# Weights loaded in half-chunks, and experts' outputs scattered as rounded float32r with their remainders

## The chip, the cores and the metric

The kernel runs on one core of one Trainium2 chip. The metric is the device time of one execution in microseconds (us). The engines are named as in the profile: PE (TensorE matmul), PEld (its weight loads), DVE (VectorE), ACT (ScalarE), POOL (GpSimd), SP (SyncE, which issues the DMAs).

## The reference

Two transformer blocks on 256 tokens of width 2048, all float32: a convolution block with a dense FFN, and a gated block that ends in a mixture of experts. The change touches the mixture (and the way that all weights are loaded). What it computes, cut to what matters:

```python
# 16 experts in 4 groups; each token goes to the 2 best experts of its best group
hid = silu(einsum('td,edf->tef', t, w_gate)) * einsum('td,edf->tef', t, w_up)     # f = 512
y = einsum('tef,efd->td', hid * gate[:, :, None], w_down)                         # d = 2048
h = h + y
return rms_norm(h, norm_final_g)
```

## The kernel before

**Streams.** All weights come from HBM once, in one fixed order, as 1 MB chunks of 128 partitions x 2048 float32 (`Stream`, lines 50 to 104). `load` issues a chunk on SP's queue into one of 4 `raw` buffers. A chunk is used as two halves of 1024 columns. Each half is split in two float32r parts: `hi`, a rounded copy on ACT (L74), and `lo`, the difference on DVE (L83; on POOL for a few early chunks). A product with a float32 weight is then two or three float32r products. When the `lo` of a chunk's second half is issued, the buffer is given back and the next chunk is loaded into it. In the mixture, `take` keeps ACT 4 halves and DVE 3 halves ahead of PE (`MOE_HI, MOE_LO`), with 5 `hi` and 4 `lo` buffers.

**The mixture** (`experts`, L1079). Each expert has 64 slots. Its stage *in e* (`into`, L1212) takes 16 halves, each with four products of 512 columns, and gathers tokens four experts at a time: while *in 3*, *in 7* and *in 11* run, PE and ACT also gather the tokens of the next four. Its stage *down e* (`down`, L1190) takes 8 halves, again with four products each; after two halves a bank of 512 columns is complete and ACT copies it to `Yt` (L1203). The order of stages is in 0, in 1, down 0, in 2, down 1, in 3, down 2, ..., in 14, down 13, down 14, in 15, down 15. Between *in e* and *down e* lie seven small jobs (`between`, L1159: gate and up out of their banks `gu` on ACT, folded by PE, silu, product, split into `hd`), done one per half in the stage that follows *in e*.

**The scatter.** `scatter(k, es)` (L1141) adds the outputs of a pair of experts (e-1, e), e even, to the tokens for one block k of 128 features: for each expert one float32 product of 256 columns, with `Yt` as weights and `sc` (slots x tokens, carrying the gate and the norm) as the moving side, then one DVE addition into `h` (L1148). Experts 0 and 15 are scattered alone. The 16 scatters of a pair wait in `todo`; `fill` puts them on PE after the products of a half, so far as a credit of 0.5 us per half goes (`FILL_GU`, `FILL_DOWN`). `sc` is made per expert in `spread` (L1126) by two DVE instructions.

**Order.** Every engine executes its own instructions in the order in which the code emits them. `beat` (L1091) emits for each half: ACT's `hi` and DVE's `lo` that run ahead, then all that was posted before (reads of banks), then one job of `between`; then come PE's products of the half. So an ACT copy out of a bank stands in ACT's queue behind `hi` casts of later halves, which wait for their DMAs.

Of the kernel before, what the change touches and what calls it, by code (L numbers as in the profile page):

```python
# [7 lines left out]
F32 = mybir.dt.float32  # L8
F32R = mybir.dt.float32r
# [6 lines left out]
P = 128  # L16
# [24 lines left out]
RAW_BUFS, HI_BUFS, LO_BUFS = 4, 5, 4  # L41
# [7 lines left out]
class Stream:  # L49
# [9 lines left out]
    def load(self, upto):  # L59
        while self.loaded < min(upto, len(self.order)):  # L60
            t = self.raw.tile([P, 2048], F32, tag="raw", name=f"raw{self.loaded}")
            self.nc.sync.dma_start(out=t, in_=self.order[self.loaded][0])
            self.raws[self.loaded] = t
            self.loaded += 1

    def source(self, half):
        i, s = divmod(half, 2)
        self.load(i + 1)
        return self.raws[i][:, s * 1024 : (s + 1) * 1024]
# [8 lines left out]
    def low_to(self, halves):  # L78
        while self.n_low < halves:
            i, s = divmod(self.n_low, 2)  # L80
            eng = self.nc.gpsimd if self.order[i][1] else self.nc.vector
# [50 lines left out]
def network(ctx, tc, a, out):  # L132
# [62 lines left out]
    y = const.tile([P, KB, T], F32, name="y")  # L195
# [754 lines left out]
    lt = wE.tile([20, T], F32, name="lt")  # L950
# [125 lines left out]
    yx = wE.tile([P, 8, T], F32, name="yx")  # L1076
    Yt = [t.rearrange("p a t -> p (a t)") for t in (y[:, :8, :], y[:, 8:, :], yx)]

    def experts(hot, stream, extra):  # L1079
        scat, rsl, hids, left = {}, {}, {}, [0] * NE  # L1080
# [45 lines left out]
        def spread(e):  # L1126
# [4 lines left out]
            sc = wF.tile([P, T], F32, tag="sc", bufs=5, name=f"sc{e}_{turn_of[0]}")  # L1131
            rs = wF.tile([P, 1], F32, tag="rs", name=f"rs{e}_{turn_of[0]}")
# [6 lines left out]
            scat[e], rsl[e] = sc, rs  # L1139
# [198 lines left out]
```

## Time and profile before

| | us |
|---|---|
| median of 3 runs (2280.13 to 2283.72) | 2283.22 |
| the profiled execution | 2283.07 |
| its span | 2281.3 |

| engine, whole span | busy us | share |
|---|---|---|
| PE | 2219.8 | 97% |
| DVE | 1596.8 | 70% |
| ACT | 1255.5 | 55% |
| POOL | 214.6 | 9% |

Up to about 1680 us the kernel is dense (convolution, FFN, projections); the mixture with its 192 chunks takes from 1680 to 2260, the final norm and output the rest. The busy time of an engine is the union of its instructions; a wait is put down to the instruction that ended it. PE's matmuls are pipelined, so the cost of one is read from the distance between starts, not from its duration.

### The profile page before, as it was taken

How to read it: one execution, taken by the hardware profiler on the slowest of the kernel's cores; microseconds unless marked ns; L12 is line 12 of the kernel's file. 1: busy time of each engine (PE TensorE's matmuls, PEld its weight loads, DVE VectorE, ACT ScalarE, POOL GpSimd, SP SyncE). 2: the span in 40 equal slices, each digit the busy share in tenths (PEclk: the TensorE clock that was granted, in tenths of full speed). 3: DMA queues.
4: the chain of work that ended last, by engine and by line, in shares of the span. 5: the costliest groups of instructions: out<-in, count | busy, mean ns of one | idle time of the engine just before them, and what ended most of it. 6: DMA issues, size and time to landing. Idle time of an engine off the chain costs nothing. (4 is left out here: it accounts for less than half of the span.)

```text
span 2281.3 us, 40365 instructions
## 1 busy us (share of the span) xinstructions
PE 2219.8 (97%) x16539; PEld 2079.1 (91%) x16539; DVE 1596.8 (70%) x2259; ACT 1255.5 (55%) x1638; POOL 214.6 (9%) x162
## 2 busy tenths in 40 slices
PE   6999999999999999999999999999999999999996
PEld 6999899999999999999899999999976878778785
DVE  7999767655544455555875664566579899888996
ACT  4445555544434444444553444444577878778774
POOL 5798100000000000001100000000000000000001
PEclk8999999999999999999999999999999999999998
DMA  5444354555555555555655555555559999999993
GB/s 212 167 166 161 101 202 167 187 200 188 200 188 200 189 198 191 191 198 188 222 185 196 193 185 188 198 190 201 169 205 367 355 351 355 331 348 344 354 357 135
DMA packets 71410, 508.79 MB, mean 223 GB/s; under 512 B 7936, under 2 KB 7952, under 8 KB 10288
## 3 DMA queue, kind: packets, MB, share of 16 engines
q1 hardware_dynamic: 70560, 503.85, 62.3%
q8 instruction: 131, 2.15, 0.4%
q0 software_dynamic: 656, 2.27, 0.3%
q14 instruction: 63, 0.52, 0.1%
HBM read 503.99 MB, written 2.10 MB: 222 GB/s over the span
## 5 line engine op out<-in xcount | busy, mean ns | idle before, releaser
L83 DVE TENSOR_TENSOR lo<-raw,hi 128x1024 fp32r<-128x1024 f32 x884 | 1064.1, 1222 | 534.4 <-PE bank L165 471.9
L74 ACT CAST hi<-raw 128x1024 fp32r<-128x1024 f32 x952 | 986.4, 1054 | 770.5 <-PE bank L165 674.6
L165 PE MATMUL bank<-aH,hi 128*128 128x256 f32 (+1 forms) x3456 | 965.4, 280 | 7.1 <-ACT aH L244 5.3
L165 PE MATMUL bank<-aL,hi 128*128 128x256 f32 (+1 forms) x3456 | 960.0, 279 | 8.0 <-DVE aL L246 8.0
L165 PE MATMUL bank<-aH,lo 128*128 128x256 f32 (+1 forms) x3456 | 962.6, 279 | 0.4 <-DVE lo L83 0.4
L165 PEld LDWEIGHTS bank<-aH,hi 128*128 128x128 f32 x3456 | 652.7, 189 | 10.1 <-ACT aH L244 5.7
L165 PEld LDWEIGHTS bank<-aL,hi 128*128 128x128 f32 x3456 | 649.8, 189 | 9.5 <-DVE aL L246 9.3
L165 PEld LDWEIGHTS bank<-aH,lo 128*128 128x128 f32 x3456 | 652.4, 189 | 0.6 <-DVE lo L83 0.6
L536 POOL TENSOR_TENSOR acc<-acc,sq 128x256 f32<-128x256 f32 x23 | 17.7, 768 | 1925.3 <-ACT sq L677 722.9
L165 PE MATMUL bank<-hidH,lo 128*128 128x256 f32 x704 | 194.3, 276 | 0.0
L165 PE MATMUL bank<-hidH,hi 128*128 128x256 f32 x704 | 194.3, 276 | 0.0
L165 PE MATMUL bank<-hidL,hi 128*128 128x256 f32 x704 | 194.3, 276 | 0.0
L83 POOL TENSOR_TENSOR lo<-raw,hi 128x1024 fp32r<-128x1024 f32 x68 | 163.4, 2415 | 52.8 <-ACT hi L74 33.1
L285 DVE SCALAR_TENSOR_TENSOR bank<-glu,vec,bank 128x256 f32<-128x256 f32 x387 | 160.6, 483 | 1.9
L165 PEld LDWEIGHTS bank<-hidH,hi 128*128 128x128 f32 x704 | 132.2, 188 | 0.0
L165 PEld LDWEIGHTS bank<-hidL,hi 128*128 128x128 f32 x704 | 132.2, 188 | 0.0
L165 PEld LDWEIGHTS bank<-hidH,lo 128*128 128x128 f32 x704 | 132.2, 188 | 0.0
L165 PE MATMUL bank<-hi,aH 128*128 128x512 f32 x320 | 128.8, 419 | 1.1 <-ACT hi L74 0.8
L165 PE MATMUL bank<-hi,aL 128*128 128x512 f32 x320 | 126.2, 411 | 0.0
L165 PE MATMUL bank<-lo,aH 128*128 128x512 f32 x320 | 123.3, 401 | 2.0 <-DVE lo L83 2.0
L165 PE MATMUL bank<-hi,hd_first 128*128 128x512 f32 x256 | 112.3, 439 | 0.1
L165 PE MATMUL bank<-lo,aL 128*128 128x512 f32 x256 | 103.3, 404 | 1.7 <-DVE lo L83 1.4
(284 smaller groups left out, 2181.9 us busy)
## 6 DMA issues: line engine op xcount, KB each, us to landing
raw<-egu SPq DMA_DIRECT2D x128, 1024.0 KB, 5.2
raw<-gu SPq DMA_DIRECT2D x88, 1024.0 KB, 4.8
raw<-w SPq DMA_DIRECT2D x72, 1024.0 KB, 4.8
raw<-edn SPq DMA_DIRECT2D x64, 1024.0 KB, 5.8
raw<-dn SPq DMA_DIRECT2D x44, 1024.0 KB, 4.8
raw<-cw_in SPq DMA_DIRECT2D x32, 1024.0 KB, 4.8
raw<-cw_out SPq DMA_DIRECT2D x16, 1024.0 KB, 4.8
raw<-wup SPq DMA_DIRECT2D x16, 1024.0 KB, 4.8
```

The costliest lines, as they stand in the source:

```text
L74: self.nc.scalar.copy(hi, self.source(self.n_high))
L83: eng.tensor_tensor(lo, self.source(self.n_low), self.highs[self.n_low].bitcast(F32), OP.subtract)
L165: nc.tensor.matmul(o, l, r, start=start, stop=stop, skip_group_check=True)
L285: nc.vector.scalar_tensor_tensor(dw[:, j, :] if t == end - 1 else ta, gl, V("w_dw", j * TAPS + t), early[j % 2] if t == 1 else ta, OP.mult ...
L536: (nc.gpsimd if n or gpsimd else nc.vector).tensor_tensor(acc[:, n, :], acc[:, n, :], sq, OP.add)
```

## The change

It has three parts.

1. `Stream` loads halves (512 KB, 128 x 1024, rows of 4 KB out of rows of 8 KB) into 8 `raw` buffers instead of chunks into 4; a buffer is given back after the `lo` of its own half.
2. An expert's output is rounded to float32r when ACT copies it out of its bank to `Yt`. Half a step later PE adds, by a product with minus the identity, minus the rounded value to the bank, so that the bank keeps the remainder, and ACT copies the 64 rows that matter to `yl` (a pair shares it: one expert in rows 0 to 63, the other in 64 to 127; `hd` is laid out accordingly). A scatter does two feature blocks in one bank, all float32r: per block one product for each expert and one for both remainders, then one DVE addition of 512 columns.
3. `sc` becomes a matrix of 0 and 1; the gate goes into ACT's copy of `gu` instead. `spread` makes three DVE instructions of its two, and ACT copies half of `sc` to `both`, the moving side of the remainders. `Yt` has two buffers in the place of three, in the room of `y`; `FILL` credits are charged 0.72 for two blocks of a pair, where one block was charged 0.86.

```diff
-RAW_BUFS, HI_BUFS, LO_BUFS = 4, 5, 4
+RAW_BUFS, HI_BUFS, LO_BUFS = 8, 5, 4
...
+            t = self.raw.tile([P, 1024], F32, tag="raw", name=f"raw{self.loaded}")
+            self.nc.sync.dma_start(out=t, in_=self.order[i][0][:, s * 1024 : (s + 1) * 1024])
...
+            del self.raws[self.n_low]
             self.n_low += 1
-            if s == 1:
-                del self.raws[i]
-                self.load(i + 1 + RAW_BUFS)
+            self.load(self.n_low + RAW_BUFS)
...
             def scale():
-                nc.vector.scalar_tensor_tensor(sc, o[:, :T], slot_col, rb, OP.is_equal, OP.mult, accum_out=rs)
-                nc.vector.tensor_tensor(sc, o[:, T:], sc, OP.mult)
+                nc.vector.scalar_tensor_tensor(scaled, o[:, :T], slot_col, rb, OP.is_equal, OP.mult, accum_out=rs)
+                nc.vector.scalar_tensor_tensor(scaled, scaled, 1.0, o[:, T:], OP.mult, OP.mult, accum_out=gs)
+                nc.vector.tensor_scalar(sc, o[:, :T], slot_col, None, OP.is_equal)
+                nc.scalar.copy(pairs[e][high_rows(e), :], sc[high_rows(e), :].bitcast(F32))
...
         def scatter(k, es):
             b, o = spare()
-            for n, e in enumerate(es):
-                mm(o[:, :T], Yt[e % 3][:, k * P : (k + 1) * P], scat[e], n == 0, n == len(es) - 1)
-                left[e] -= 1
+            rows = slice(0, P) if len(es) == 2 else high_rows(es[0])
+            for kk in (k, k + 1):
+                sl, to = slice(kk * P, (kk + 1) * P), o[:, kk % 2 * T : (kk % 2 + 1) * T]
+                for n, e in enumerate(es):
+                    mm(to, Yt[e % 2][:, sl], scat[e], kk == k and n == 0, False)
+                mm(to, yl[rows, sl], pairs[es[0]][rows, :], False, True)
...
             def add():
-                nc.vector.tensor_tensor(h[:, k, :], h[:, k, :], o[:, :T], OP.add)
+                two = h[:, k : k + 2, :]
+                nc.vector.tensor_tensor(two, two, o.rearrange("p (a t) -> p a t", a=2), OP.add)
...
-                nc.scalar.copy(gu[:, 1, :], bank[1])
+                nc.scalar.activation(gu[:, 1, :], bank[1], ACT.Copy, scale=gsl[e])
...
-                        def out_of_bank(c=c, o=o):
-                            nc.scalar.copy(Yt[e % 3][:, c * 512 : (c + 1) * 512], o)
+                        def out_of_bank(c=c, o=o, sl=sl):
+                            nc.scalar.copy(Yt[e % 2][:, sl], o)
+                            post(lambda: lost(c, o, sl))
+                        def lost(c, o, sl):
+                            mm(o, minus, Yt[e % 2][:, sl], False, True)
+                            nc.scalar.copy(yl[rows, sl], o[rows])
                             es = (e,) if e in (0, NE - 1) else (e - 1, e)
                             if e == NE - 1 or e % 2 == 0:
-                                for k in range(4 * c, 4 * c + 4):
-                                    todo.append((0.43 * len(es), lambda k=k: scatter(k, es)))
+                                for k in (4 * c, 4 * c + 2):
+                                    todo.append((0.24 * (len(es) + 1), lambda k=k: scatter(k, es)))
```

**Where the instructions stand.** On PE in *down 6*, a stage whose pair begins to be scattered, before: `bank_62` and `bank_63` take the expert's output, `bank_66` and `bank_67` the scatters. Here the third and fourth halves:

```order
L165 MATMUL bank_63<-hi_20836,hd_first 128x512
L165 MATMUL bank_63<-lo_20856,hd_first 128x512
L165 MATMUL bank_66<-sc_first,yx 128x256
L165 MATMUL bank_66<-sc_first,y 128x256
L165 MATMUL bank_67<-sc_first,yx 128x256
L165 MATMUL bank_67<-sc_first,y 128x256
L165 MATMUL bank_63<-hi_20854,hd_first 128x512
```

The same place after:

```order
L164 MATMUL bank_63<-lo_21730,hd_first 128x512
L164 MATMUL bank_62<-Yt_first,minus 128x512
L164 MATMUL bank_63<-hi_21728,hd_first 128x512
L164 MATMUL bank_63<-lo_21743,hd_first 128x512
L164 MATMUL bank_63<-hi_21728,hd_first 128x512
L164 MATMUL bank_63<-lo_21743,hd_first 128x512
L164 MATMUL bank_66<-sc_first,Yt_first 128x256 x2
L164 MATMUL bank_66<-both_first,yl 128x256
L164 MATMUL bank_66<-sc_first,Yt_first 128x256 x2
L164 MATMUL bank_66<-both_first,yl 128x256
```

A product with `minus` now stands between two halves, and the scatters begin one half later, two blocks to a bank. Counted over the program, a *down* of an even expert (2 to 12) holds 5 blocks of a pair before and 10 after, the next *in* 9 and 6, the *down* of the odd expert behind it 2 and none; three `minus` products stand in each *down* and the fourth in the *in* that follows.

On ACT in the same stage, before, from the copies of `gu` on:

```order
L1164 COPY gu_first<-bank_61 128x512
L74 CAST hi_20865<-raw_20778 128x1024
L74 CAST hi_20879<-raw_20778 128x1024
L1203 COPY y<-bank_62 128x512
L74 CAST hi_20896<-raw_20806 128x1024
L1177 ACTIVATE sg_first<-bank_64 128x256
L74 CAST hi_20909<-raw_20806 128x1024
```

After:

```order
L1185 ACTIVATE gu_first<-bank_61,gs_first 128x512
L75 CAST hi_21741<-raw_21628 128x1024
L75 CAST hi_21755<-raw_21643 128x1024
L1228 CAST Yt_first<-bank_62 128x512
L75 CAST hi_21770<-raw_21658 128x1024
L1234 CAST yl<-bank_62 64x512
L1198 ACTIVATE sg_first<-bank_64 128x256
L75 CAST hi_21795<-raw_21673 128x1024
```

Behind each copy of an output, one `hi` cast later, a second read of the same bank (L1234) has come in.

## Rows read from the trace of the kernel before

**Rows 1.** Busy time by stage, eight windows in a row less the last: us, then engines
```profile
1841.64:1861.68 20.04, 19.00 (x69) 11.59 (x68) 18.59 (x17) 16.01 (x17) 0.00 (x0) 1.00 0.99 408
1861.68:1877.44 15.76, 13.74 (x70) 11.28 (x68) 14.04 (x20) 13.29 (x18) 0.00 (x0) 1.00 0.90 334
1877.44:1901.14 23.70, 23.70 (x106) 19.41 (x105) 22.89 (x29) 16.75 (x19) 0.00 (x0) 1.00 0.97 360
1901.14:1912.31 11.17, 11.17 (x58) 9.49 (x57) 9.09 (x13) 8.77 (x14) 0.00 (x0) 1.00 0.86 293
1912.31:1936.75 24.44, 23.96 (x134) 20.11 (x132) 22.55 (x24) 24.29 (x34) 0.00 (x0) 1.00 0.98 380
1936.75:1950.81 14.06, 13.65 (x70) 11.34 (x69) 11.09 (x15) 12.15 (x18) 0.00 (x0) 1.00 0.84 297
1950.81:1974.66 23.85, 23.85 (x107) 19.46 (x105) 22.91 (x29) 16.86 (x19) 0.00 (x0) 1.00 0.96 356
```

**Rows 2.** Timeline, PE: one block of a pair's scatter between plain products
```profile
1948.34 0.60 PE L165 MATMUL bank<-sc_first,yx 128*128 128x256 f32 x2
1948.78 0.59 PE L165 MATMUL bank<-sc_first,y 128*128 128x256 f32 x2
1949.02 0.58 PE L165 MATMUL bank<-hi,hd_first 128*128 128x512 f32 x1
1949.44 0.39 PE L165 MATMUL bank<-lo,hd_first 128*128 128x512 f32 x1
```

**Rows 3.** Timeline, PE: float32r products of 512 and of 256 columns
```profile
1688.72 0.39 PE L165 MATMUL bank<-lo,aH 128*128 128x512 f32 x1
1688.95 0.40 PE L165 MATMUL bank<-hot_first,tH 128*128 128x256 f32 x2
1689.19 0.40 PE L165 MATMUL bank<-hot_first,tL 128*128 128x256 f32 x2
```

**Rows 4.** Groups of instructions by line and shape: busy us, mean ns | idle before
```profile
L1148 DVE TENSOR_TENSOR x<-x,bank 128x256 f32<-128x256 f32 x144 | 59.7, 419 | 32.6 <-PE bank L165 31.4
L847 DVE TENSOR_TENSOR vm<-bank,bsb 128x512 f32<-128x512 f32 x4 | 2.8, 689 | 2.8 <-PE bank L165 2.7
L1203 ACT COPY y<-bank 128x512 f32<-128x512 f32 x44 | 25.8, 587 | 15.2 <-PE bank L165 15.2
```

**Rows 5.** Timeline of ACT and PE at the beginning of *down 4*
```profile
1862.24 1.99 ACT L74 CAST hi<-raw 128x1024 fp32r<-128x1024 f32 x2 [0.72 <-DVE sc_first L1135]
...
1864.14 0.68 ACT L1163 ACTIVATE gu_first<-bank,rs_first 128x512 f32<-128x512 f32 x1
...
1864.87 1.16 PE L165 MATMUL bank<-fold,gu_first 128*128 128x128 f32 x8 [2.02 <-ACT gu_first L1163]
```

**Rows 6.** Timeline of ACT, copy of an output in *down 6*
```profile
1944.88 0.59 ACT L1203 COPY y<-bank 128x512 f32<-128x512 f32 x1 [1.66 <-PE bank L165]
```

**Rows 7.** Timeline of ACT and of DVE in *in 7*, where `sc` is made
```profile
1932.87 1.14 ACT L74 CAST hi<-raw 128x1024 fp32r<-128x1024 f32 x1
...
1933.76 0.48 DVE L1135 SCALAR_TENSOR_TENSOR sc_first<-bank,slot_col,rb 128x256 f32<-128x256 f32 x1
1934.16 0.08 DVE L1135 DVE_READ_ACCUMULATOR sc_first<-bank,slot_col,rb 128x1 f32 x1
```

**Rows 8.** Busy time in the end, from *in 15* on, columns as in rows 1
```profile
2216.27:2236.43 20.16, 20.16 (x89) 16.36 (x88) 17.99 (x23) 12.10 (x13) 0.00 (x0) 1.00 0.99 386
2236.43:2243.88 7.45, 7.39 (x42) 6.34 (x40) 4.97 (x8) 7.29 (x10) 0.00 (x0) 1.00 0.19 80
2243.88:2260.84 16.96, 15.52 (x65) 11.88 (x65) 12.72 (x24) 11.12 (x22) 8.09 (x11) 1.00 0.01 1
```

**Rows 9.** Busy time near the program's start and after a wait in *down 8*
```profile
5.80:8.00 2.20, 2.20 (x6) 1.35 (x6) 1.24 (x3) 1.44 (x5) 0.00 (x0) 1.00 1.00 371
...
2011.00:2012.00 1.00, 1.00 (x7) 1.00 (x6) 0.82 (x2) 1.00 (x2) 0.00 (x0) 0.50 0.66 246
```

**Rows 10.** Timeline of SP: issues at the program's start
```profile
5.19 2.44 SPq L62 DMA_DIRECT2D raw<-cw_in  x4
```

**Rows 11.** Waits of SP's queue between 600 and 1600 us: us, times, longest
```profile
SPq L62 <- DVE lo L83: 774.9, 154, 16.9
```

More of the change, by code (lines that the diff above doesn't have):

```diff
@@ L66, in source @@
     def source(self, half):
-        i, s = divmod(half, 2)
-        self.load(i + 1)
-        return self.raws[i][:, s * 1024 : (s + 1) * 1024]
+        self.load(half + 1)
+        return self.raws[half]
     def high_to(self, halves):
@@ L1074, in gates @@
         nc.vector.tensor_copy(nmore_i, nmore)
-    yx = wE.tile([P, 8, T], F32, name="yx")
-    Yt = [t.rearrange("p a t -> p (a t)") for t in (y[:, :8, :], y[:, 8:, :], yx)]
+    yl = wE.tile([P, 8 * T], F32R, name="yl")
+    high_rows = lambda e: slice(e % 2 * CAP, (e % 2 + 1) * CAP)
+    minus = wE.tile([P, P], F32R, name="minus")
+    nc.scalar.activation(minus, idt, ACT.Copy, scale=-1.0)
+    ctxY.close()
     def experts(hot, stream, extra):
-        scat, rsl, hids, left = {}, {}, {}, [0] * NE
+        ctxZ = ExitStack()
+        wZ = pool("wZ", c=ctxZ, side="right")
+        Yt = [wZ.tile([P, 8 * T], F32R, name=f"Yt{n}_{turn_of[0]}") for n in range(2)]
+        scat, rsl, gsl, hids, left, pairs = {}, {}, {}, {}, [0] * NE, {}
         jobs, todo, posts, credit, ring = deque(), deque(), deque(), [0.0], deque((6, 7))
@@ L1147, in add @@
+            for e in es:
+                left[e] -= 2
             def add():
-                nc.vector.tensor_tensor(h[:, k, :], h[:, k, :], o[:, :T], OP.add)
+                two = h[:, k : k + 2, :]
+                nc.vector.tensor_tensor(two, two, o.rearrange("p (a t) -> p a t", a=2), OP.add)
                 if NE - 1 in es:
-                    post(square)
-            def square():
-                sq = square_to(k)
-                nc.scalar.activation(sq, h[:, k, :], ACT.Square)
-                post(lambda: add_square(sq, k, True))
+                    for kk in (k, k + 1):
+                        post(lambda kk=kk: square(kk))
@@ L1157, in scatter, with square @@
+            def square(kk):
+                sq = square_to(kk)
+                nc.scalar.activation(sq, h[:, kk, :], ACT.Square)
+                post(lambda: add_square(sq, kk, True))
             post(add, b)
@@ L1177, in silu @@
                 nc.scalar.activation(sg, view(0), ACT.Silu)
+            first, second = (slice(n * CAP, (n + 1) * CAP) for n in (e % 2, 1 - e % 2))
             def high():
-                nc.scalar.copy(hd[:, :, :CAP], sg)
+                nc.scalar.copy(hd[:, :, first], sg)
                 if e == NE - 1:
@@ L1187, in between @@
                     high,
-                    lambda: nc.vector.tensor_tensor(hd[:, :, CAP:], sg, hd[:, :, :CAP].bitcast(F32), OP.subtract)])
+                    lambda: nc.vector.tensor_tensor(hd[:, :, second], sg, hd[:, :, first].bitcast(F32), OP.subtract)])
         def down(e):
-            while e >= 3 and left[e - 3] > 0:
+            while e >= 2 and left[e - 2] > 0:
                 todo.popleft()[1]()
@@ L1259, in experts @@
                 posts.popleft()()
+        ctxZ.close()
+        ctxO = ExitStack()
+        last = pool("wO", c=ctxO, side="right").tile([P, KB, T], F32, name=f"last_{turn_of[0]}")
         natural_sums(bank[2], 2, lone)
@@ L1265, in experts @@
         for k in range(KB):
-            nc.vector.scalar_tensor_tensor(y[:, k, :], h[:, k, :], V("final", k), bank[3][:, :T], OP.mult, OP.mult)
+            nc.vector.scalar_tensor_tensor(last[:, k, :], h[:, k, :], V("final", k), bank[3][:, :T], OP.mult, OP.mult)
             if k in (1, 3, 7, 11, 15):
                 k0 = {1: 0, 3: 2}.get(k, k - 3)
-                nc.sync.dma_start(out=out[:, k0 : k + 1, :], in_=y[:, k0 : k + 1, :])
+                nc.sync.dma_start(out=out[:, k0 : k + 1, :], in_=last[:, k0 : k + 1, :])
+        ctxO.close()
     experts(hot, stream, gates())
```

22 lines of the change are left out of this document (12 added, 10 removed).

## The prediction

> **What bounds the kernel now.** I read the busy time by stage first, because the mixture is where the change works and its stages have different limits [rows 1]. One turn over four experts stands there: in 5, down 4, in 6, down 5, in 7, down 6, in 8; the eighth, down 7, is like down 5 (11.15 us). The reader should look for the engine whose busy time equals the stage's length.
>
> - *in* of an even expert (23.70 and 23.85 us; six such, 4 to 14): PE is busy for all of it. But DVE is busy for 22.89 of the 23.70, so it is only 0.8 us behind.
> - *down* of an odd expert (11.17 us): PE, all of it. DVE 9.09, ACT 8.77.
> - *in 7*, with its gathers (24.44 us; three such): ACT, 24.29.
> - *in 5*, without gathers or scatters (20.04 us; 5, 9 and 13): no engine is full (DVE 18.59, PE 19.00 with few instructions); DMA shows 0.99 at 408 GB/s.
> - *down* of an even expert (15.76 and 14.06 us): the first holds a wait of PE, below; the second is PE, 13.65.
>
> So PE holds about half of the mixture's time, but nowhere is the next engine far. Before 1680 us nothing should move: SP there waits for free buffers (774.9 us in 154 waits [rows 11]), so weights are loaded as soon as there is room, and well ahead of PE.
>
> **The change, part by part.** *Prices.* A block of a pair's scatter costs PE 0.87 us: without it the `hi` product would start at 1948.34 and the next `lo` 0.23 later, at 1948.57, and it starts at 1949.44 [rows 2]. A float32r product costs 0.23 us for 512 columns, and two of 256 columns cost 0.24, so 0.12 each [rows 3]. The new block has three of those, 0.36. DVE's addition is 0.419 us for 256 columns, so 0.838 for two blocks, and 0.689 for one operation of 512 columns out of a bank [rows 4]. The new `sc` costs DVE one more operation on 256 columns (nearest: 0.419 [rows 4]) and one more read of the accumulator (0.08 [rows 7]): +0.5 per expert. ACT's new copy of a remainder has 64 rows and 512 columns; the nearest row is 0.587 for 128 rows [rows 4]. It could be less, hardly more; I take 0.5, four per expert. The two operations that ACT adds per expert for `both` and the scaled `gu` I take as 0.4 and 0.1, with the 0.587 as upper bound for each.
>
> *in, even expert (six).* It loses 9 blocks at 0.87 and gets 6 at 0.36 (how many stand where is told with the change) and one product with minus the identity: PE 23.70 - 7.83 + 2.16 + 0.23 = 18.3 us. PE is then no longer the limit. DVE: 22.89 - 9 x 0.419 + 3 x 0.689 + 0.5 = 21.7. DMA: 16 halves of 0.524 MB at the 408 GB/s of *in 5* [rows 1] are 20.6. I take 21.4, close to DVE, a little less since DVE comes in with a lead when PE has waited in the stage ahead. That is -2.3 each, **-13.8**; ends: 20.6 (-3.1 each) and DVE's old 22.9 (-0.8 each), if its additions come no cheaper.
>
> *down, odd expert (five with scatters).* PE loses two blocks and gets three minus products: 11.17 - 1.74 + 0.69 = 10.1. But PE now arrives without being behind, and then the wait of *down 4* is to be expected here too: the fold of `gu` waited 2.02 us for ACT, whose copy stood behind two `hi` casts that waited for their weights [rows 5]. Half of that eats the gain: 11.2, **0**; ends -1 and +1 each, 5 us either way.
>
> *down, even expert (six).* Five blocks before, ten after, three minus products: -4.35 + 3.6 + 0.69, no change for PE. DVE gets 5 x 0.689 - 5 x 0.419 = +1.35 (14.04 to 15.4, under the 15.76), ACT three remainders and 0.1 (12.15 to 13.75, under the 14.06): both are hidden, but barely. The new wait is that of the minus product: it needs ACT's copy of the output. Behind it on PE stand all later halves, and behind those the scatters. Before, ACT came to that copy early and waited 1.66 us for PE [rows 6]; a copy behind late casts would cost up to a fold's 2.02. I take 0.25 per stage, **+1.5**; ends 0 and +12.
>
> *in with gathers (three).* ACT is the limit and gets a remainder (0.5), `both` (0.4), and a wait: its `hi` cast ends at 1934.0 [rows 7], DVE would end the three operations of `sc` at about 1935.2 (they begin at 1933.76 [rows 7] and take 0.48 + 0.08 [rows 7] + 0.42 [rows 4] now, 0.5 more after), and `both` waits for them, with the gathered copies behind it. 0.5 + 0.4 + 1.2 = 2.1; I take 2.0, **+6.0**; ends +2.5 (the operations alone, some of them covered) and +6.5.
>
> *in 5, 9, 13.* DMA sets them. Buffers come back half a chunk earlier, rows are half as long. No row has 4 KB rows; near the start rows of 2.1 and 2.8 KB moved at 371 GB/s [rows 9], against 408 for 8 KB. By that the ends are +0.7 each (half of the way to 371) and -1.2 each (DVE's 18.6 becomes the limit). **-1.0** for the three.
>
> *The end.* in 15 carries scatters (20.16 us), its DMA is at 0.99: -0.7. The 7.45 us of jobs behind it were filled with scatters on PE and keep their own chain: -1.0. In the last *down* [rows 8] PE had 32 products (7.5 us) and 16 single blocks (16 x 0.43 = 6.9) in 16.96; after, 7.5 + 4 x 0.23 + 8 x 0.48 = 12.3, with the same 2.6 of gaps 14.9: -2.1. A last remainder adds about 1 us of latency (copy, product, copy), the shorter scatters behind it give as much back. PE in down 13 and 14 has 7 blocks less at 0.87 and 10 more at 0.36 and 7 minus products: 0.9 less, of which I count -0.7. Together **-4.5**, ends -7 and -1.
>
> *Issues.* SP issues four in 2.44 us [rows 10], 0.61 each; 24 halves per expert are 15 us of about 36. Hidden, even doubled in the dense part.
>
> *Sum.* -13.8 + 0 + 1.5 + 6.0 - 1.0 - 4.5 = -11.8. From the profiled execution's 2283.07 that is 2271.3; the median of the runs is 0.15 above it, which changes nothing.
>
> A rule of the skill speaks against part 1. The Trainium skill, "DMA: Bandwidth & Descriptors", section "Bandwidth", asks for transfers of 1 MiB and more, and the section "Anatomy of one DMA" fits 2 us plus the bytes at 436 GB/s, by which 512 KB alone would be an estimated 3.2 us, 77 us per expert. The trace disagrees as far as that goes, since eight transfers of 272 KB queued together ran at 371 GB/s; what is left of the rule is the fourth rival.
>
> **The rivals.** *Leads carry over.* If the buffers smooth the stages, the average decides. Over the turn of 144.2 us DVE is busy 130.2 [rows 1] (down 5 counted twice); after, four experts need 4 x 0.5 more for `sc` and 16 x 0.689 - 32 x 0.419 = -2.4 for additions, so about 130; ACT's 117 becomes about 127. With 2% of loss that is 132.5 per turn, 11.7 less, -41 on 3.5 turns and -45 with the end. Two thirds of that is what I give as this case: about 2253. Against it: ACT is full in *in 7* alone, and 4 or 5 halves of buffers do not carry over from there.
>
> *Another engine is already there.* DVE is at 97% in the stages that gain most. If these go to 22.2 only (-1.5 each, -9), the gathers cost 6, the even *down* 1.5, and the end gives 2, the sum is -4.5 with the -1.0: 2279, within the noise. (That the new scatter is not cheaper is a weak form of it: rows 3 show its products at their price.)
>
> *Slower: the minus product holds PE.* Eleven *down* stages with four such waits are set by PE, so each microsecond counts. A mean wait w costs 44 w, against the 11.8 gained (with the 1.5 taken out, 13.3): it decides from w = 0.3 us. At 0.6 the sum is +13, 2296. For it: the 2.02 us of rows 5, and that after a wait of this kind the granted clock fell to 0.50, the lower of the two levels, 1.2 GHz [rows 9]. Against it: the 1.66 us by which ACT was early [rows 6], and one whole half of PE's work that stands between the copy and the minus product.
>
> *Slower: short rows load slower.* If halves come at 371 GB/s, 16 of them are 22.6 us: 1.2 more in each of six, 2.4 in each of three stages, +14, about 2286; worse if the rate is lower, so I count 2290.
>
> **How the numbers follow.** Forecast 2271 (2263 to 2278): 0.42. Leads carry over, 2253: 0.17. Another engine, 2279: 0.16. Minus product, 2296: 0.18. Short rows, 2290: 0.07. The ends of the terms together reach from 2251 to 2303, but not all at once; with a half of the outer two cases left out the range is 2253 to 2293. About 0.2% (4.6 us) is what a measurement of this kernel can tell from no change: faster than that 0.59 (the first two), within 0.18 (the third and the edges of the others), slower 0.23.
>
> **What would show it.** In the profile after: *in* of even experts at 21 to 22 us with DVE full and PE waiting for `lo` (right), or at 23 or more (wrong). Odd *down* stages at about 11, with a wait of PE for `gu`. *in 7* longer by 2, with ACT waiting for DVE at `both`. Waits of PE for the copy into `Yt` under 0.3 us in the mean; if they are longer, the third rival. DMA in *in 5* at 400 GB/s or more; if under 380, the fourth. Up to 1680 us no more than 1 us of difference; if the dense part moves, the claim that loads are covered there is wrong.

## The result, and the profile after

The changed kernel is slower: 2318.03 us (median of four, 2312.07 to 2320.06) against 2281.68 of the kernel before beside it, a ratio of 1.0147 with a 95% interval of 1.0131 to 1.0164. (Ratios are given as they are on record; the quotient of the two medians, 1.0159, lies within the interval.) The span of the profiled execution is 2318.2 us, 36.9 more than before. The prediction was 2271 with a range up to 2293.

The table compares stage lengths, from the first product of a stage on PE to the first of the next, means over the stages of a kind.

| stages (how many) | before | after | predicted, all | measured, all |
|---|---|---|---|---|
| even *in*, 4 to 14 (6) | 23.75 | 19.82 | -13.8 | -23.6 |
| odd *down*, 3 to 11 (5) | 11.16 | 16.40 | 0 | +26.2 |
| even *down*, 2 to 12 (6) | 15.18 | 17.10 | +1.5 | +11.5 |
| *in* with gathers (3) | 25.28 | 25.35 | +6.0 | +0.2 |
| *in* 5, 9, 13 (3) | 20.36 | 18.86 | -1.0 | -4.5 |
| *down* 13 and 14 together | 24.18 | 30.96 | -0.7 | +6.8 |
| *in 15* with its jobs | 27.61 | 25.64 | -1.7 | -2.0 |
| last *down* to the end | 37.42 | 43.89 | -2.1 | +6.5 |
| *in 0*, *in 1*, *down 0*, *in 2*, *down 1* | | | not costed | +15.8 |
| sum | | | -11.8 | +36.9 |

Every *in* stage that had a forecast kept or beat it. The loss lies in the *down* stages and at the two ends of the mixture. Of the 15.8 that were not costed, *down 0* has 6.5, *down 1* 6.4 and *in 0* and *in 1* together 3.4; the last is not clear of noise, since *down 0* begins anywhere from 1719 to 1724 us in runs of kernels with half-chunks.

Busy time by stage after, the same turn as in [rows 1] and with its columns (in 5, down 4, in 6, down 5, in 7, down 6):

```profile
1858.78:1877.64 18.86, 17.96 (x71) 12.11 (x69) 17.06 (x15) 16.14 (x18) 0.00 (x0) 1.00 0.91 312
1877.64:1897.74 20.10, 16.63 (x83) 14.20 (x82) 15.48 (x22) 15.28 (x23) 0.00 (x0) 0.83 0.87 332
1897.74:1917.56 19.82, 19.72 (x90) 14.45 (x89) 19.79 (x22) 15.17 (x17) 0.00 (x0) 1.00 0.95 334
1917.56:1934.27 16.71, 12.56 (x52) 9.35 (x51) 12.95 (x17) 14.01 (x20) 0.00 (x0) 0.90 0.96 365
1934.27:1959.63 25.36, 24.41 (x134) 20.13 (x133) 20.67 (x22) 24.10 (x35) 0.00 (x0) 1.00 0.93 332
1959.63:1974.93 15.30, 13.74 (x83) 11.84 (x82) 12.85 (x15) 14.42 (x23) 0.00 (x0) 1.00 0.82 268
```

*in 6* went as forecast: DVE is busy for 19.79 of 19.82 us, and PE's weight loads wait for `lo` there, 2.4 us in 6 places. In *down 5* (16.71 us, 11.17 before) no engine is full: ACT is the fullest with 14.01, where it had 8.77. The granted clock of the two *down* stages that are longest is 0.83 and 0.90.

Outside the mixture nothing moved. In 1080 us of the dense part PE is busy for all but 0.8 us, and from 1720 us on the mean clock is 0.96 (before, 0.98 in the same window, and 1.00 up to 2260 us):

```profile
600.00:1680.00 1080.00, 1079.21 (x9238) 1063.92 (x9237) 622.79 (x786) 495.14 (x626) 17.93 (x40) 1.00 0.60 190
1720.00:2280.00 560.00, 501.99 (x2322) 383.83 (x2322) 484.02 (x528) 468.06 (x597) 0.00 (x0) 0.96 0.91 328
```

Waits from 1720 to 2275 us (who <- for whom: us in total, times, longest). One of the kernel before:

```profile
PE bank L165 <- ACT gu_first L1163: 8.4, 8, 2.0
```

After:

```profile
PE bank L164 <- ACT gu_first L1184: 35.7, 15, 3.5
ACT both_first L1149 <- DVE sc_first L1148: 28.5, 15, 3.8
ACT yl L1234 <- PE bank L164: 21.5, 31, 1.7
PE bank L164 <- ACT Yt_first L1228: 14.9, 22, 0.9
```

In the same part of the kernel before, PE waited 8.4 us in 8 places for the copy of `gu`; it is 35.7 in 15 now, once per expert but one. The row below it is new: ACT waits once per expert for DVE's `sc`, to copy it into `both`.

The two belong together, as the timeline at the beginning of *down 5* shows (lines of other instructions are left out):

```profile
1916.90 0.50 DVE L1146 SCALAR_TENSOR_TENSOR scaled_first<-bank,slot_col,rb 128x256 f32<-128x256 f32 x1
1917.78 0.48 DVE L1148 TENSOR_SCALAR sc_first<-bank,slot_col 128x256 fp32r<-128x256 f32 x1
1918.30 0.41 ACT L1149 CAST both_first<-sc_first 64x256 fp32r<-64x256 f32 x1 [2.87 <-DVE sc_first L1148]
1918.61 1.99 ACT L75 CAST hi<-raw 128x1024 fp32r<-128x1024 f32 x2
1920.50 0.68 ACT L1184 ACTIVATE gu_first<-bank,rs_first 128x512 f32<-128x512 f32 x1
1921.23 1.16 PE L164 MATMUL bank<-fold,gu_first 128*128 128x128 f32 x8 [2.60 <-ACT gu_first L1184]
```

ACT stands 2.87 us for `sc`, which DVE makes behind `lo` parts of its own. Then come, in ACT's order, the copy into `both` (0.41), two `hi` casts (1.99) and the copy of `gu` (0.68), and PE's fold starts as that ends, 2.60 us late. Two microseconds later the granted clock is at 0.50:

```profile
1923.00:1924.00 1.00, 1.00 (x4) 0.79 (x3) 0.94 (x1) 0.63 (x1) 0.00 (x0) 0.50 1.03 422
```

At the two ends of the mixture, experts 0 and 15 are scattered alone. The timeline of PE in *down 0*:

```profile
1733.90 0.38 PE L164 MATMUL bank<-both_first,yl 64*128 64x256 f32 x1
1734.21 0.39 PE L164 MATMUL bank<-sc_first,Yt_first 128*128 128x256 f32 x1
1734.53 0.38 PE L164 MATMUL bank<-both_first,yl 64*128 64x256 f32 x1
1734.84 0.38 PE L164 MATMUL bank<-sc_first,Yt_first 128*128 128x256 f32 x1
```

Products of 64 rows alternate with products of 128, and each starts 0.31 us after the one before it. In the scatter of a pair, in *down 4*, all have 128 rows, and a product costs 0.12 (three in 0.35):

```profile
1890.00 0.40 PE L164 MATMUL bank<-sc_first,Yt_first 128*128 128x256 f32 x2
1890.23 0.28 PE L164 MATMUL bank<-both_first,yl 128*128 128x256 f32 x1
1890.35 0.40 PE L164 MATMUL bank<-sc_first,Yt_first 128*128 128x256 f32 x2
```

### The profile page after: what moved, and what is told of

It is laid out like the page before. It is cut to its first block, busy times and chain, and to the rows that moved or that the text cites. A ratio compares the mean times of both kernels' runs of the same rounds, so it can differ in the third digit from the quotient of the medians.

```text
span 2318.2 us, 41701 instructions
## 1 busy us (share of the span) xinstructions
PE 2216.2 (96%) x16491; PEld 2060.5 (89%) x16491; DVE 1600.5 (69%) x2219; ACT 1299.5 (56%) x1719; POOL 213.9 (9%) x162
## 4 chain that ended last, share of the span: by engine, by line
PE 87%; ACT 6%; DVE 3%; issue 2%; DMA 1%; DVEq 0%; SPq 0%; ACTq 0%
PE bank L164 87%; ACT hi L75 4%; DVE lo L83 1%; DMA raw<-edn 1%; ACT Yt_first L1228 1%; DVE bank L395 1%; ACT yl L1234 0%; DVE u L242 0%; ACT gu_first L1184 0%; DVE aL L246 0%; ACT aH L1028 0%; DVE last_first L1301 0%; PE bank L167 0%; DMA x<-x 0%; DVE sc_first L1148 0%
## 5 line engine op out<-in xcount | busy, mean ns | idle before, releaser
L164 PE MATMUL bank<-hi,aH 128*128 128x512 f32 x320 | 122.0, 398 | 0.2 <-ACT aH L562 0.2
```

What stands on the lines that cost most here:

```text
L164: nc.tensor.matmul(o, l, r, start=start, stop=stop, skip_group_check=True)
```

## The experiments

Each edit was made to the changed kernel unless said otherwise. Ratios are to runs of the kernel before on the same chip, intervals are 95%. The runs were made in batches on different chips, on which the kernel before took 2281.7 to 2283.7 us; a difference between medians of two batches is uncertain by a microsecond or two for that alone. The chip time of the two kernels and of the eighteen with an edit stands first, with stage means as in the table above:

| kernel | median us | ratio | odd *down* | even *down* | even *in* | *down* 13+14 |
|---|---|---|---|---|---|---|
| before | 2281.7 | 1 | 11.16 | 15.18 | 23.75 | 24.18 |
| the change | 2318.0 | 1.0147 | 16.40 | 17.10 | 19.82 | 30.96 |
| e1_half_only | 2276.0 | 0.9977 | 11.17 | 14.78 | 23.75 | 24.19 |
| e4_full_chunks | 2326.1 | 1.0182 | 16.62 | 17.14 | 19.83 | 30.95 |
| e2_both_later | 2293.7 | 1.0047 | 14.54 | 15.93 | 19.82 | 28.42 |
| e5_both_pool | 2282.2 | 0.9995 | 12.98 | 15.68 | 19.81 | 28.08 |
| e3_no_remainder | 2280.7 | 0.9990 | 13.60 | 14.92 | 21.12 | 25.07 |
| e7_pool_no_remainder | 2249.8 | 0.9859 | 10.57 | 12.93 | 21.11 | 22.61 |
| f1_no_minus | 2275.9 | 0.9967 | 11.98 | 14.58 | 20.28 | 27.80 |
| f2_no_yl_copy | 2261.3 | 0.9918 | 12.00 | 14.83 | 19.82 | 23.86 |
| e6_idle_products | 2303.7 | 1.0088 | 15.13 | 16.18 | 19.80 | 29.35 |
| e9_pool_idle | 2285.2 | 1.0016 | 13.77 | 15.68 | 19.81 | 28.62 |
| e8_yl_on_dve | 2297.1 | 1.0053 | 13.40 | 16.45 | 20.53 | 28.77 |
| e12_reads_first | 2302.2 | 1.0097 | 13.76 | 16.29 | 20.95 | 27.74 |
| e13_pool_casts | 2277.7 | 0.9987 | 13.19 | 14.66 | 20.39 | 26.37 |
| e14_pool_casts_idle | 2282.4 | 1.0003 | 13.19 | 15.00 | 20.41 | 26.35 |
| f3_dve_odd | 2283.8 | 1.0010 | 12.91 | 15.16 | 19.81 | 27.43 |
| f4_dve_odd_pool | 2284.2 | 1.0007 | 12.91 | 14.98 | 20.41 | 28.58 |
| f5_full_rows | 2308.6 | 1.0111 | 15.79 | 16.62 | 19.81 | 30.96 |
| f6_pool_casts_full | 2275.5 | 0.9969 | 13.28 | 14.65 | 20.40 | 26.37 |

### The half-chunks: e1 and e4

`e1_half_only` is the kernel before with part 1 alone; `e4_full_chunks` is the changed kernel with the 1 MB chunks and four buffers of before. Of the edit of the first, which is part 1 as shown with the change, one line:

```diff
-RAW_BUFS, HI_BUFS, LO_BUFS = 4, 5, 4
+RAW_BUFS, HI_BUFS, LO_BUFS = 8, 5, 4
```

> The kernel before with part 1 alone: half-chunk transfers into 8 buffers. If the shorter rows cost the time, this is 2295 to 2315. If the loss sits in the queues of ACT and PE behind the new copies, part 1 is harmless or a small gain: 2272 to 2284, with the stages in 5, 9 and 13 at 19 us instead of 20.

> The changed kernel with the transfers of before: 1 MB chunks into 4 buffers. If half-chunks cost time: 2285 to 2300. If they help a little or not at all: 2318 to 2330.

Alone, the half-chunks gain: 0.9977 (0.9964 to 0.9989). Taken out of the changed kernel they cost it 8.1 us more, 1.0182 (1.0156 to 1.0207) against 1.0147, whose interval just overlaps with it. So part 1 is worth some 7 us in the kernel before and likely as much in the changed one, a part of it in *in* 5, 9 and 13 (20.36 to 19.30 in `e1_half_only`), and it is not where the time went.

### The copy into `both`: e2 and e5

`e2_both_later` leaves the copy on ACT, but posts it, so that it is issued one half later. `e5_both_pool` gives it to POOL.

```diff
-                nc.scalar.copy(pairs[e][high_rows(e), :], sc[high_rows(e), :].bitcast(F32))
+                post(lambda: nc.scalar.copy(pairs[e][high_rows(e), :], sc[high_rows(e), :].bitcast(F32)))
```

```diff
-                nc.scalar.copy(pairs[e][high_rows(e), :], sc[high_rows(e), :].bitcast(F32))
+                nc.gpsimd.tensor_copy(pairs[e][high_rows(e), :], sc[high_rows(e), :].bitcast(F32))
```

> The changed kernel with one edit: ACT's copy into both is emitted one half later, so that DVE has made sc by then. If the in-order wait of that copy (28.5 us in 15 places) is what holds up the copies of gu and through them PE's fold (35.7 us in 15 places, 8.9 before), the fold waits fall under 15 us together and the time to 2283 to 2295. If the minus product is the cause, the time stays within 5 us of 2318.

> The changed kernel with the copy into both made by POOL (idle in the mixture) in the place of ACT. If ACT's place in the queue is the cause, this frees it fully: the fold waits come under 20 us together and the time to 2285 to 2292, a little under the kernel where ACT's copy is only emitted later (2293.7). If it was ACT's extra work that mattered and not the wait, the same 0.4 us per expert is gained, 6 us: 2312.

`e2_both_later` took 2293.7 us, 24 less than the change, though PE's wait for `gu` came to 22.6 us only and not to under 15, and `e5_both_pool` 2282.2, 36 less: level with the kernel before (0.9995, 0.9986 to 1.0005). One copy of 0.41 us per expert, moved to an engine that was idle, is worth nearly the whole loss. The waits of `e5_both_pool`, 1720 to 2265 us:

```profile
PE bank L164 <- ACT Yt_first L1228: 15.6, 23, 0.9
PE bank L164 <- ACT gu_first L1184: 14.0, 14, 3.0
```

The wait for `gu` fell from 35.7 to 14.0. The timeline where its *down 5* begins (other lines left out):

```profile
1900.98 0.48 DVE L1148 TENSOR_SCALAR sc_first<-bank,slot_col 128x256 fp32r<-128x256 f32 x1
1901.07 0.68 ACT L1184 ACTIVATE gu_first<-bank,rs_first 128x512 f32<-128x512 f32 x1
1901.52 1.32 POOL L1149 CAST both_first<-sc_first 64x256 fp32r<-64x256 f32 x1 [35.41 <-DVE sc_first L1148]
1901.80 0.97 PEld L164 LDWEIGHTS bank<-fold,gu_first 128*128 128x128 f32 x8 [0.42 <-ACT gu_first L1184]
1901.81 1.16 PE L164 MATMUL bank<-fold,gu_first 128*128 128x128 f32 x8
```

ACT copies `gu` at 1901.07, before `sc` is even done; POOL waits for `sc`, takes three times as long as ACT (1.32), and nobody waits for it. The weights of the fold wait 0.42 us for that copy, where the fold waited 2.60.

### The remainders: e3, e7, f1 and f2

`e3_no_remainder` has no remainders at all (no product with `minus`, no copy to `yl`, no product with `yl`); `e7_pool_no_remainder` is that with `both` on POOL. `f1_no_minus` and `f2_no_yl_copy` are `e5_both_pool` without the one half or the other: without the product, `yl` holds whole outputs; without the copy, `yl` stays zero.

```diff
-                            mm(o, minus, Yt[e % 2][:, sl], False, True)
-                            nc.scalar.copy(yl[rows, sl], o[rows])
```

> The changed kernel without the remainders: the product with minus the identity, ACT's copy into yl and the products with yl are left out, so the output lacks what the rounding of an expert's output loses; the copy into both stays. If the wait at both is the main cause, the fold waits stay near 35 us and only the waits for Yt (14.9 us on PE) and part of the 64 x 0.23 us of products go: 2290 to 2305. If the minus product is the main cause: 2270 or less, under the kernel before.

> POOL's copy into both, and the remainders left out (product with minus the identity, copy into yl, products with yl), so the output lacks what the rounding loses. Both suspected causes are gone: if they are all of the loss, this shows the whole gain of the cheap scatter, 2250 to 2262. If the two causes overlap (each alone gave 24 and 37 of the 35 us), it stays near 2275.

> POOL's copy into both (2282.2), and the product with minus the identity left out while ACT's copy into yl and the products with yl stay, so yl holds whole outputs and the result counts them twice. ACT's load is unchanged, PE has no wait for Yt in the stage. If that wait (15 us on PE) with its 15 us of products is what is left, 2252 to 2262; if ACT's load in down is, 2274 to 2282.

> POOL's copy into both, and ACT's copy into yl left out while the product with minus the identity stays; yl is zero, so the output lacks the remainders. PE still waits for Yt, ACT has 64 copies less (about 32 us). If PE's wait is what is left, 2275 to 2282; if ACT's load is, 2252 to 2262.

Without remainders the change takes 2280.7 us, 37 less; with `both` on POOL too 2249.8, 68 less, and 1.4% faster than the kernel before. So the copy and the remainders cost about the same (36 and 37 us), and one hardly hides the other (73 against 68 together). `e3_no_remainder` lies between its two forecasts, and its waits from 1720 to 2265 us are the change's own, so what it gained is another cost than the late fold:

```profile
PE bank L164 <- ACT gu_first L1183: 35.1, 15, 3.1
ACT both_first L1149 <- DVE sc_first L1148: 27.0, 15, 4.6
```

In `e7_pool_no_remainder` an odd *down* takes 10.57 us, less than the 11.16 of before.

Of the 32.4 us between `e5_both_pool` and `e7_pool_no_remainder`, the product with minus the identity is worth 6.3 (`f1_no_minus`), and ACT's copy to `yl` 20.9 (`f2_no_yl_copy`); the rest is the products with `yl` and what holds only together. The groups of the changed kernel, 1720 to 2275 us, show what that copy is (busy us, mean ns | idle before):

```profile
L1228 ACT CAST Yt_first<-bank 128x512 fp32r<-128x512 f32 x60 | 35.0, 583 | 7.9 <-PE bank L164 7.4
L1234 ACT CAST yl<-bank 64x512 fp32r<-64x512 f32 x60 | 34.9, 582 | 22.0 <-PE bank L164 21.5
L1149 ACT CAST both_first<-sc_first 64x256 fp32r<-64x256 f32 x15 | 6.1, 404 | 28.5 <-DVE sc_first L1148 28.5
```

It takes 64 rows and costs as much as the copy of 128 (582 and 583 ns): 34.9 us of ACT in 60 copies, and another 22.0 us in which ACT stands idle ahead of it, nearly all of that for PE. Without it the wait of PE for `gu` stays, and the wait for `Yt`, 15.6 in `e5_both_pool`, nearly goes (rows of `f2_no_yl_copy`, 1720 to 2265 us):

```profile
PE bank L164 <- ACT gu_first L1185: 14.7, 15, 1.8
PE bank L164 <- ACT Yt_first L1229: 3.4, 8, 0.9
```

So its price is ACT's load, by which ACT comes late with `Yt` and PE's product with `minus` waits, and not one more late fold. It isn't confined to the *down* stages: of the 25.6 us between the two profiled spans some 16 lie there, and 7 in the *in* stages 3, 5, 7, 9, 11 and 13. With the product left out and the copy kept, PE's wait only moves to that copy (`f1_no_minus`, same window):

```profile
PE bank L164 <- ACT yl L1233: 11.2, 11, 1.4
```

### The clock: e6, e9 and e14

`e6_idle_products` puts eight products of the identity, into a bank that nobody reads, ahead of the first fold. `e9_pool_idle` and `e14_pool_casts_idle` do it with six, on `e5_both_pool` and on `e13_pool_casts` (below).

```diff
             def folded(g):
+                if g == 0:
+                    idle_products(bank[4][:, :P], 8)
```

> The changed kernel with 8 products of the identity with itself put ahead of the first fold of each expert on PE, 128 x 128 float32, about 2 us of work that nothing reads. PE waits there for 2.4 us in the mean. If the granted clock's fall behind these waits is a part of the loss (0.96 in the mean from 1720 to 2280 us, 1.00 before), the clock stays at 1.00 there and the time falls by 8 to 20 us, to 2298 to 2310. If the waits alone are the loss, the time is the same or up to 5 us longer.

> POOL's copy into both (2282.2 alone) and 6 products of the identity with itself ahead of the first fold. If the granted clock's fall behind the fold waits is a part of its own, some 20 of the fold's microseconds being left, the time is 2268 to 2276, under the kernel before; if POOL's copy has already taken the clock's part away (0.99 in the mean there), it is 2279 to 2284.

> As before this one, with 6 idle products ahead of the first fold. If load and clock are separate parts, 3 to 8 us less than without them; if not, the same within 3 us.

In the change the idle products gained 14.3 us (2303.7), though they are work added to PE. PE's timeline in *down 5* of `e6_idle_products`, and its busy time there:

```profile
1911.70 1.95 PE L164 MATMUL bank<-idt 128*128 128x128 f32 x16
1914.44 1.16 PE L164 MATMUL bank<-fold,gu_first 128*128 128x128 f32 x8 [0.79 <-ACT gu_first L1184]
```

```profile
1910.76:1925.89 15.13, 12.80 (x69) 9.91 (x67) 12.87 (x17) 13.93 (x20) 0.00 (x0) 1.00 1.01 404
```

(The trace has two records for each of these float32 products, hence x16.) The fold begins 3.68 us after the stage does (1910.76), as late as in the change (1917.56 to 1921.23), but the clock stays at 1.00 for the whole stage. So some 14 us of the loss were the fall of the clock behind the fold's wait. The changed kernel shows the price by itself: *down 7* kept the clock, and *down* 3, 5, 9 and 11, at 0.90, took 16.65 to 16.74 us; with the idle products all five take 15.12 to 15.16.

```profile
1994.75:2009.91 15.16, 11.04 (x53) 7.98 (x51) 12.53 (x15) 13.95 (x20) 0.00 (x0) 1.00 1.00 377
```

(The expectation's 1.00 for the kernel before holds up to 2260 us; in its window to 2280 it is 0.98.) Where the wait is short the products only cost: 2285.2 against 2282.2 of `e5_both_pool`, and 2282.4 against 2277.7.

### Other places for ACT's work: e8, e12, e13, f3 and f4

All five have `both` on POOL, as `e5_both_pool`. `e8_yl_on_dve` lets DVE copy to `yl`. `e12_reads_first` lets `beat` emit the posted reads of banks before the `hi` casts that run ahead. `e13_pool_casts` gives two of the eight `hi` casts of a *down* to POOL. `f3_dve_odd` replaces, for odd experts, product and copy by one subtraction on DVE, and `f4_dve_odd_pool` adds POOL's casts in the even *down* stages.

```diff
-                            nc.scalar.copy(yl[rows, sl], o[rows])
+                            nc.vector.tensor_copy(yl[rows, sl], o[rows])
```

```diff
-            got = stream.half()
             for _ in range(len(posts)):
                 posts.popleft()()
+            got = stream.half()
```

```diff
+            if self.order[self.n_high // 2][1] == "hi" and self.n_high % 2:
+                self.nc.gpsimd.tensor_copy(hi, self.source(self.n_high))
+            else:
                 self.nc.scalar.copy(hi, self.source(self.n_high))
```

```diff
+                            if e % 2:
+                                nc.vector.tensor_tensor(yl[rows, sl], o[rows], Yt[e % 2][rows, sl].bitcast(F32), OP.subtract)
+                            else:
                                 mm(o, minus, Yt[e % 2][:, sl], False, True)
                                 nc.scalar.copy(yl[rows, sl], o[rows])
```

> POOL's copy into both, and the copy of the remainder into yl by DVE in the place of ACT. If the down stages are set by ACT's own work (8 casts, 4 + 4 copies, gu, silu and high: 14.2 us, which is the length of an odd down once both is out of the way), they fall to 12 to 13 us and the time is 2270 to 2282; DVE gets 4 x 0.69 us per expert. If the minus product's wait is set by the order of the queues and not by ACT's load, they stay at 14.

> POOL's copy into both, and in every half the posted reads of banks are emitted ahead of the casts and differences that run ahead. ACT's copy into Yt then stands ahead of a hi cast and not behind it. If the minus product waits because of the order in ACT's queue, its waits (about 15 us on PE) go and the odd down falls from 13 to 11 us: 2260 to 2270. If ACT's load in down is the cause, the wait moves to the hi casts and the time is 2278 to 2295.

> POOL's copy into both, and 2 of the 8 hi casts of each down made by POOL in the place of ACT. If ACT's load in down is what is left (8 casts, 8 copies, gu, silu and high are 14.2 us), 2 us of it go per down: odd down 11 to 12.5 us and 2255 to 2270. If the order of the queues is the cause, or POOL's cast is so slow (2.4 us for its differences) that PE waits for it, the time is 2280 or more.

> POOL's copy into both, and for odd experts the remainder made by one DVE subtraction out of the bank in the place of product and copy (nothing left out). Odd downs have no scatters and DVE has about 2 us to spare there. If both parts of the remainder matter and DVE's time is free there, odd downs fall to 11.5 us and the time to 2265 to 2275; if DVE is the limit as with all remainders on DVE (2297), 2285 to 2292.

> As before this one, with 2 of the 8 hi casts made by POOL in the even downs. If the gains add (2277.7 for POOL's casts in all downs), 2260 to 2272; if POOL's casts slow DVE's differences down (1.49 us each beside a cast, 1.17 without), no better than without them.

On DVE the copy lost 15 us: in 520 us from 1720 on DVE is then busy for 500.36, and ACT's relief is worth nothing.

```profile
1720.00:2240.00 520.00, 479.30 (x2258) 362.23 (x2258) 500.36 (x567) 421.16 (x504) 18.11 (x14) 0.99 0.94 344
```

Reads first lost 20 us: the even *in* stages went from 19.81 to 20.95, and *in* 5, 9 and 13 from 18.86 to 20.14, and DVE waited 50.0 us for casts, where it was 29.7 in `e5_both_pool`: the casts now stand behind reads that wait for PE. PE's wait for `Yt` stayed (14.5 us of 15.6), so emitting that copy ahead of the casts doesn't take the wait away. The odd remainders on DVE changed nothing, alone (2283.8) or with POOL's casts (2284.2): what the even *down* stages gave went back in *in* 5, 9 and 13 (20.07 and 19.98, from 18.86). POOL's casts took 4.5 us off, but the intervals of the two ratios overlap (0.9974 to 1.0000, and 0.9986 to 1.0005), so that this is a gain isn't shown. Even *down* stages became shorter (15.68 to 14.66), a part of that went back in the even *in* (19.81 to 20.39), and the odd *down*, for which 11 to 12.5 was expected, didn't gain (12.98 to 13.19): in *down 5* DVE, slower beside POOL (last section), is busy for all of the 13.19 us.

### All rows in the lone scatters: f5 and f6

`f5_full_rows` lets the scatters of experts 0 and 15 contract all 128 rows, the other half being zero. `f6_pool_casts_full` is that on `e13_pool_casts`.

```diff
-            rows = slice(0, P) if len(es) == 2 else high_rows(es[0])
+            rows = slice(0, P)
```

> The changed kernel with one edit: the scatters of the two experts that stand alone (0 and 15) contract all 128 rows of yl and both, whose other half is zero, instead of 64 rows, so every product of a scatter has one shape. The same 32 products per expert stay. In the changed kernel's trace a product of these scatters begins 0.31 us after the one before it, and in the pairs' scatters 0.12 us. Theory that the mix of shapes costs the 0.19 us: 64 products x 0.19 = 12.2 us at the most, less what DVE's and ACT's emptying of the banks then bounds (0.45 us per product of emptying in the pairs' scatters by the row of the stage in 5): 2305 to 2312. Rival that the products of these two stages are spaced by who empties the banks, or by the load of weights, and not by their shape: 2316 to 2320, and the spacing stays at 0.31.

> The changed kernel with the copy into both on POOL, two of every eight hi casts of a down stage on POOL, and all 128 rows in the scatters of experts 0 and 15. Without the last edit it took 2277.7. If the mix of shapes costs 0.19 us per product at both ends: 2264 to 2271, faster than both kernels. Rival that the two ends are held by the emptying of the banks or by transfers: 2275 to 2279.

The spacing is a matter of shape. The same eight products in *down 0* now start 0.12 us apart:

```profile
1734.58 0.28 PE L164 MATMUL bank<-sc_first,Yt_first 128*128 128x256 f32 x1
1734.69 0.29 PE L164 MATMUL bank<-both_first,yl 128*128 128x256 f32 x1
1734.82 0.28 PE L164 MATMUL bank<-sc_first,Yt_first 128*128 128x256 f32 x1
1734.94 0.28 PE L164 MATMUL bank<-both_first,yl 128*128 128x256 f32 x1
```

`f5_full_rows` took 2308.6 us, 9.5 less. Its profiled span fell by 11.0. At the two places themselves 5.9 went: *down 0* fell from 21.89 to 17.47, *in 2* rose from 19.59 to 20.05, and from the last *down* to the end it is 41.95 in the place of 43.89. The other 5.1 are *down* stages that came out shorter where nothing was edited (3, 4 and 11 by 1.6, 1.7 and 1.6, 12 by 1.0, 8 by 0.2), less 0.9 by which *down 0* began later. But for *down 8*, the clock fell less in these: *down 3* in the change and here,

```profile
1842.05:1858.78 16.73, 12.61 (x52) 9.35 (x51) 12.53 (x15) 14.02 (x20) 0.00 (x0) 0.90 0.96 372
1839.03:1854.20 15.17, 11.05 (x53) 7.98 (x51) 12.55 (x15) 13.94 (x20) 0.00 (x0) 1.00 1.03 410
```

while PE's wait for `gu` is the same (35.5 us in 15 places, 35.7 in the change). Why the clock held there stays open, so these 5 us can't be put down to the rows. At the end, a part of what the spacing freed went into a wait of PE for `Yt` (1.99 us before the last product with `minus`, 0.63 in the change).

`f6_pool_casts_full` took 2275.5, 0.9969 (0.9955 to 0.9983): faster than both kernels, by 0.3% than the one before, but only 2.2 us better than `e13_pool_casts`, which the two intervals don't tell from nothing. Its end is 2.7 shorter (40.84 against 43.56). *down 0* is 2.3 shorter too (15.50 against 17.84), but *in 2* behind it took 1.05 back, and of the rest only 0.3 is left when the last *down* begins. `e1_half_only`, part 1 alone, reaches the same time.

## Why the prediction was wrong

**What held.** The dense part didn't move. Short rows didn't load slower, and the fourth rival is out: part 1 gains 7 us. The sign that was named for it would have misled: *in 5* shows 312 GB/s, under the 380, in a stage that became shorter, and halves moved at 414 elsewhere (last section). SP's issues are hidden. The new scatter of a pair costs PE 0.35 us per block, as priced. The even *in* stages went to DVE as the limit, and further than said: 19.82, not 21.4, because DVE's 19.79 are less than the 21.7 of the sum: a part of its work moved into the *down* behind. *in* 5, 9 and 13 gained 1.5 each, where 0.33 was forecast. These are the -28.1 us of the table. One bound was mis-sized, and nothing hung on it: half of the way from 408 to 371 GB/s is 1.0 us for 16 halves, not 0.7. The Trainium skill, "DMA: Bandwidth & Descriptors", section "Anatomy of one DMA", gives the fit that is quoted against part 1 for transfers of the gpsimd path. These weights are issued by SP, and no run here times one such transfer alone.

**The step that failed first: `both` was costed in three stages.** The prediction saw that the copy waits for DVE, with 1.2 us of wait and 0.4 of work, but put it into *in 7* and its like alone, because ACT is the limit there. `sc` is made once per expert, at the end of every *in*, and [rows 5] said so: ahead of the fold's wait of 2.02, ACT's own cast stood 0.72 us for `sc` L1135. What is queued behind the waiting copy on ACT was named as the gathered copies; it is two casts and the copy of `gu`, for which PE waits. The faster *in* makes it worse, because DVE is the limit there and comes to `sc` late. In *in 6* before, `sc` was done 2.4 us ahead of the stage's end at 1901.14:

```profile
1898.29 0.42 DVE L1136 TENSOR_TENSOR sc_first<-bank,sc_first 128x256 f32<-128x256 f32 x1
```

In the change it is done 0.7 us into *down 5* (1918.26, in the timeline of the section on the result). So the gather stages got +0.07 each in the place of +2.0, and the *down* stages got the wait: 28.5 us of ACT, 35.7 of PE. Moving the copy gave 36 us back.

**The second: ACT wasn't summed for the odd *down*.** The term there was PE's 10.1 and half of a fold wait, 11.2. The same sum for ACT is 8.77 [rows 1] + 3 x 0.5 + 0.1 + 0.4 = 10.8 by the prediction's own prices: more than PE's 10.1. It came to 14.01 in 20 instructions (14 before), for ACT also comes in with less done ahead: *in 6* holds 17 of its instructions after and 19 before [rows 1]. The prediction made this sum for the even *down* stages only and called it "hidden, but barely" there. With `both` out of the way they still take 15.68 and 12.98; without remainders 12.93 and 10.57. The remainder of 64 rows was priced at 0.5 each and costs 0.582, a small miss; that its place on ACT was taken as free was the large one. The whole is 32 us, 21 of it ACT's copy alone.

**The third rival: right side, for the larger part another mechanism.** PE does wait for `Yt`, 14.9 us in 22 of 60 products, 0.25 in the mean over all, below the 0.3 from which the rival decides, but ten times the 1.5 that stood for it in the sum. Taking the product away gave 6.3 us only, for PE then waits for the copy to `yl`; taking that copy away took 12 of the 15.6 us of the wait. So the wait is real and comes with ACT's load, and the time came out on the slow side by that and, before it, by the wait behind `both` in the same engine's queue.

**The second rival, DVE, is the next limit.** From *in 5* to *in 9* DVE is busy for 148.8 us before, 148.5 after and 148.3 in `e7_pool_no_remainder`, the fastest of all, where it fills both *in 6* and *down 5*:

```profile
1868.47:1889.58 21.11, 19.99 (x82) 13.30 (x81) 21.07 (x24) 15.12 (x16) 0.00 (x0) 1.00 0.95 329
1889.58:1900.54 10.96, 9.50 (x49) 7.74 (x48) 10.96 (x14) 10.77 (x16) 1.32 (x1) 1.00 1.02 417
```

Together they are 32.07 us, 34.87 before [rows 1]. An even *in* of 19.82 is therefore no gain by itself: in `e5_both_pool` the *down 5* behind it is full with DVE too (12.54 of 12.54, row in the last section).

**The clock** stood in the prediction as a reason for the third rival, with its row [rows 9], and not in a term. It fell to 0.50 behind the fold's waits, and keeping PE busy over them gave 14.3 us.

**The ends.** The lone scatters were priced at 0.48 us for four products, from the 0.12 of a row with one shape only; they start 0.31 apart. *down 0* was not costed at all. Of the 64 x 0.19 = 12.2 us that this would be by the spacing, `f5_full_rows` gave 5.9 back at the places themselves.

**Open.** The experiments overlap: `both` 36, remainders 37, the clock 14 and the rows 9.5 make 97, where 68 us lie between the change and `e7_pool_no_remainder`. The clock's 14 are a part of what the first gives, since idle products on top of `e5_both_pool` gain nothing, and the rows' 9.5 are a part of the remainders, since no product of 64 rows is left without them. Which share of the remainders' last 5 us (32.4 less 6.3 and 20.9) is the products with `yl` was not told apart.

## What to carry to other kernels

Before an instruction is given to an engine that "has room", write down what is queued behind it on that engine and who waits for the last of these; an in-order queue hands the wait on, here 0.41 us of copy as 2.60 us of PE. Sum the load of every engine stage by stage, the short stages first: the share over the whole turn left ACT room, and the *down* stage had almost none. Where one engine's work can be put off, count neighbouring stages together: what an *in* stage gained here came back in part as DVE's work in the *down* behind it. An idle engine, even one three times as slow, is the right place for a copy that nobody needs soon.

## What the runs showed of the hardware

- Float32r products that alternate between 64 and 128 rows start 0.31 us apart, and with all 128 rows 0.12, both for 256 columns. Whether 64 rows alone or the change of shape costs it was not told apart.
- A copy out of a bank costs ACT the same for 64 rows as for 128 (582 and 583 ns for 512 columns).
- After PE had waited 2.60 us in *down 5*, the clock was granted at 0.50, the lower of its two levels (1.2 GHz); products without a use, put into that wait, kept it at 1.00.
- Halves of 512 KB with rows of 4 KB moved at 414 GB/s in *down 5* of `e5_both_pool`, as fast as the 408 of the 8 KB rows in [rows 1]:

```profile
1900.74:1913.28 12.54, 10.99 (x53) 7.97 (x51) 12.54 (x17) 12.17 (x18) 1.32 (x1) 1.00 1.03 414
```

- POOL's casts slow DVE beside them. In DVE's timeline of `e13_pool_casts` four `lo` subtractions in a row take 1.15 us each with POOL idle, and six that follow 1.49 each, with POOL at work in half of that time:

```profile
1892.68 4.61 DVE L86 TENSOR_TENSOR lo<-raw,hi 128x1024 fp32r<-128x1024 f32 x4
...
1898.48 8.92 DVE L86 TENSOR_TENSOR lo<-raw,hi 128x1024 fp32r<-128x1024 f32 x6
```
